# Eight PSUM banks divided anew in a two-layer diffusion backbone: three for the score products, none for transposes alone

## The chip, the cores and the metric

The kernel runs on one core of a Trainium2 chip. The metric is the time on the device in microseconds (us), the median of several executions. The text speaks of the core's engines by the profile's names: PE is TensorE (matmuls and transposes, results in PSUM alone), PEld its loading of weights, DVE is VectorE, ACT is ScalarE, POOL is GpSimd, SP is the engine that issues most DMAs. PSUM has eight banks of 128 partitions by 512 float32 values in this kernel, and it uses all eight.

## What is computed

Two layers over 1024 latent tokens with a prefix of 256 context tokens, width 1024. In each layer the stream is normalized and modulated, projected, mixed by two parallel branches, gated with SiLU, projected back and added. Cut to what matters:

```
for i in range(2):
    h_lat = rms_norm(x_lat, norm_g[i]) * (1 + sc_l) + sh_l      # the same for the context
    if i == 0:   # A: global attention, 8 heads, RMS-normed and rotated q, k;  B: windowed, with a sink
        q, k, v, gate = split(h @ w_in);  q, k = rope(norm(q)), rope(norm(k))
        o = softmax(q k^T / 8 + bias) v
        y = (o * silu(gate)) @ w_out
    else:        # C: convolution module;  D: 2-D neighbourhood attention with a bias table
        ...
    x = x + g * y
return rms_norm(x_lat, final_g)
```

The output is the normalized latent stream, 1024 by 1024.

## The kernel before

Everything stands transposed, with features on the partitions and tokens along the free axis. A matmul that must be exact is written as three matmuls of split operands (`mm3`, L317 to L320: high by high, high by low, low by high), so a projection of one 128 by 512 block takes 8 x 3 = 24 matmuls into one bank.

**Stages.** First the modulation vectors and the normalization of the three token chunks; then the projections of the first head group alone ("solo"). Then layer 0's attention: 40 groups (four head groups `u` in the order 2, 3, 0, 1, ten query blocks each; 2 and 3 are branch B, 0 and 1 branch A), between whose steps the projections of the next head group are woven in as fill, and later the parts of the output projection. Then layer 1's convolution with its projections, layer 1's attention (16 groups) with more projections woven in, and the last norm.

**Order of the work.** A main generator (`attn_gen`, L392) and a fill generator are stepped by `weave` (L495): so many fill steps to so many main steps. The traced instructions carry a priority; those of the fill stand 80 places later in layer 0 (`FL`, `later`), the modulation steps 100 places (`LATE`). The framework then orders the instructions of each engine by priority and by when their inputs come in a modelled run; on the chip every engine goes through its own list in that order. Memory tiles have tags: a tag has a fixed number of buffers, and its tiles take them in turn, in the order of the program, each waiting until the buffer's last tenant is released.

**The banks.** `bank(tag, name)` (L103) takes a PSUM bank. Before, the eight banks are: `pp` two (projections: tiles `pq`, `pg`, `p1`, `po`), `mx` two (the products whose maxima are wanted), `st` two (score products), `ov` one (the product of the probabilities with V), `tr` one. While `solo` is set, a request for `pp` alternates in pairs between `pp` and `mx`.

**One group of attention.** `attn_prep` (L364) loads q, computes a bound on every query's scores (`maxes`: PE products into `mx`, DVE reductions L578, L589, L597, L1344, L1351), and then turns the negated maxima (`nmt`) with a transpose into the row layout (tile `trn`, L386 to L388), which DVE writes into rows 64 and on of `QL`. The main loop makes a score tile (`st`, L465 and L469; the second matmul adds the maxima through `QL`), ACT takes the exponential (`pf`, L477; in layer 1 DVE first adds a bias, L474), ACT casts the high part `ph` (L296), POOL or DVE subtracts for the low part `pl` (L299), and some tiles later three matmuls add to `ov` (L409 to L411).

**One head group's projection.** `proj_qkv` (L789) makes ten blocks, `pq`, each 24 matmuls; ACT copies each to `pc` (L802), a buffer for two blocks of which there are three (`PCB`). DVE and POOL normalize and rotate `pc`. Some blocks later `qk_tail` (L834) transposes the block into the tile `trk` (three transposes, L838), splits it (ACT L296 and DVE L299 into `qs`), stores q and k with two DMAs (L841, L842) and starts the loads of K and V. The last reading of a `pc` buffer is the transposes of its two blocks. `proj_gate` makes the gate blocks, `pg`.

**The other users of `tr`.** `rstd_steps` (L244) sums squares with small matmuls (`trs`); `mod_half` and `mod_half_v` (L169, L193) bring the modulation vectors into columns (`trm`), which DVE reads at L187 and L226. In the solo stage `mod_half_v` uses `ov` for it.

Of the kernel before, what the change touches and what calls it, by code (L numbers as in the profile page):

```python
# [41 lines left out]
TRV = "pp"  # L42
# [45 lines left out]
def tile_kernel(ctx: ExitStack, tc: tile.TileContext, a, out):  # L88
# [5 lines left out]
    dp = ctx.enter_context(tc.tile_pool(name="dp", bufs=1, space=DRAM))  # L94
    ps = ctx.enter_context(tc.tile_pool(name="ps", bufs=2, space=PSUM))

    BUFS = {"pp": 2, "mx": 2, "st": 2, "ov": 1, "tr": 1}
    solo = [True]
    turn = [0, 0]
    mk, mwp, hold, layer = [0], [None], [0], [0]  # L100
# [10 lines left out]
    def nm(s):  # L111
        uid[0] += 1
        return f"{s}_{uid[0]}"
# [55 lines left out]
    def mod_half(pool, l, part, j):  # L169

        pb = bank("pp", nm("pm"))
        c0 = part * 1024 + j * 512
        for d2 in range(4):
            w2 = mw_tile()
            mm0.append(SY.dma_start(w2, a["mod_w"][l, 2 * d2 * P : (2 * d2 + 2) * P, c0 : c0 + 512].rearrange("(d p) n -> p d n", d=2)))
            for d in range(2):
                dk = 2 * d2 + d
                PE.matmul(pb[0:2, :], csil[:, dk, :], w2[:, d, :], start=(dk == 0), stop=(dk == DK - 1))
        row = a0.tile([P, 512], F32, tag="ost", name=nm("mrow"), bufs=2)[0:2, :]
        SC.copy(row, pb[0:2, :])  # L180
        tr = bank("tr", nm("trm"))
        for i in range(4):
            PE.transpose(tr[:, 2 * i : 2 * i + 2], row[:, i * P : (i + 1) * P], ident[0:2, 0:2])
        trv = tr[:, 0:8].rearrange("p (i c) -> p i c", c=2)
        o = part * 8 + j * 4
        dst = modT[l][:, o : o + 4, :]
        VE.tensor_tensor(dst, trv, modb[:, l, o : o + 4, None].broadcast_to([P, 4, 2]), op=ALU.add)  # L187
        if part == 1:
            VE.scalar_tensor_tensor(gs[l][:, j * 4 : j * 4 + 4, :], dst, 1.0,
                                    normg[:, l, j * 4 : j * 4 + 4, None].broadcast_to([P, 4, 2]),  # L190
                                    op0=ALU.add, op1=ALU.mult)

    def mod_half_v(pool, l, part, j, conds):  # L193
# [26 lines left out]
            yield  # L220
        o = part * 8 + j * 4
        for n_, (q, t) in enumerate(zip(conds, accs)):
            tr = bank("ov" if solo[0] else "tr", nm("trm"))
            for i in range(4):
                PE.matmul(tr[:, 2 * i : 2 * i + 2], t[:, i * P : (i + 1) * P], one, start=True, stop=True)
            VE.tensor_tensor(modT[l][:, o : o + 4, q], tr[:, 0:8].rearrange("p (i c) -> p i c", c=2)[:, :, 0],  # L226
                             modb[:, l, o : o + 4], op=ALU.add)
            if part == 1:
                js = slice(j * 4, j * 4 + 4)
                VE.scalar_tensor_tensor(gs[l][:, js, q], modT[l][:, o : o + 4, q], 1.0, normg[:, l, js],  # L230
                                        op0=ALU.add, op1=ALU.mult)
# [9 lines left out]
        VE.scalar_tensor_tensor(r[:, :n], t[:, :n], 1.5, r[:, :n], op0=ALU.add, op1=ALU.mult)  # L241
        return r

    def rstd_steps(pool, accs, n, tag, inv=1.0, tr="tr"):  # L244


        nb = n // P
# [116 lines left out]
    def attn_prep(pool, g):  # L364
# [18 lines left out]
            VE.tensor_tensor(nmt[:, 8:12], se, nmt[:, 4:8].bitcast(F32), op=ALU.subtract)  # L383
        for _ in range(3):
            yield
        tr2 = bank("tr", nm("trn"))  # L386
        PE.transpose(tr2[0:nr, 0:P], nmt[:, 0:nr].bitcast(F32), ident)
        VE.tensor_tensor(QL[64 : 64 + nr, :].rearrange("p (h q) -> p h q", h=4),  # L388
                         tr2[0:nr, None, 0:P].broadcast_to([nr, 4, P]),
# [262 lines left out]
    with ExitStack() as p0x:  # L652
# [6 lines left out]
        with tc.tile_pool(name="st0", bufs=1, reuse_waits="tile") as st0:  # L659
# [30 lines left out]

            def norm_bc(c, acc):
                n = CHUNKS[c][1]
                return run(rstd_steps(st0, [acc], n, "st"))[:, :n]

            made = [0]
            accs, bcs, mh = [], [], [(0, 0), (0, 1), (1, 0), (1, 1)]
# [136 lines left out]

        def qk_tail(u, j, pc):  # L834

            tr = bank("tr", nm("trk"))
            for i in range(3):
                PE.transpose(tr[:, i * P : (i + 1) * P], pc[:, i * P : (i + 1) * P], ident)  # L838
            qs = ap.tile([P, 2, 384], F32R, tag="qs", name=nm("qs"), bufs=2)
# [130 lines left out]
    with tc.tile_pool(name="o0", bufs=1, reuse_waits="tile", side="right") as op_:  # L970
# [47 lines left out]
        accs = {}  # L1018
# [46 lines left out]
        weave(main, O1[2], chain(load_oh(parts[1]), out0_part(parts[1])), 30, False)  # L1065
        ws = [load_w(op_, a["ev_wo"], e2 * 256, 256, 256, WO, lambda dk: "gv"[dk % 2], dks=final, rb=2) for e2 in range(4)]
        fp = [final_proj(c) for c in range(3)]
        nh = [norm_h(0, "st", "tr"), norm_h(1, "pp", "tr"), norm_h(2, "st", "tr")]
        weave(main, NSTEP[U1 // 2] - O1[0] - O1[1] - O1[2], through_attention(), O1[3])
        a0x.close()  # L1070
        solo[0] = True
# [27 lines left out]
    with ExitStack():  # L1099
# [25 lines left out]
        def ln_steps(vp, c):  # L1125
# [23 lines left out]
                    VE.tensor_tensor(s1, s1, sq, op=ALU.add)  # L1149
                yield  # L1150
            yield
            bc = yield from rstd_steps(vp, [s1], 512, "st", 2.0)
            SC.copy(s2, bc)
            yield
            for i in range(4):
# [478 lines left out]
```

## Time and profile before

| | |
|---|---|
| median of three executions | 1557.82 us (1554.83 to 1560.38) |
| profiled execution | 1555.72 us, span of its instructions 1553.9 us |
| mean granted clock of TensorE | 0.967 |
| moved by DMA | 221.01 MB |

The profiled execution lies 2.1 us under the median of the three. The profile gives for each engine the busy time, the waits by what ended them, and the instructions in order of time. "PE st L465 <- ACT pf L477: 16.5, 17, 2.3" reads: PE stood idle ahead of the matmul of line 465 that writes `st`, and what ended the wait was ACT's instruction of line 477 that writes `pf`; 16.5 us in total, 17 times, 2.3 us the longest. In a table of windows each engine has its busy time and the number of its instructions, then follow the granted clock of TensorE as a share of full speed, the share of DMA time and GB/s.

### The profile page before, as it was taken

To read this page: it belongs to the slowest core of one execution; us is meant where nothing else is said; L and a number is where in the kernel's file an instruction comes from. 1 tells how busy PE (TensorE), PEld (TensorE's weight loads), DVE (VectorE), ACT (ScalarE), POOL (GpSimd) and SP (SyncE) were. 2 spreads that over 40 slices of the span, in tenths; PEclk is the share of its full clock that TensorE was granted. 3 is DMA by queue.
4 is the path that set the end of the run, shared out by engine and by line. 5 is a ranking of instruction groups with operands and counts; after the bars stand their busy time and mean duration, and the time that the engine had idled before them with its cause. 6 is when DMAs were issued, how large, how long until landed. Compare 5 with 4: busy or idle time off the path is not lost.

```text
span 1553.9 us, 22052 instructions
## 1 busy us (share of the span) xinstructions
PE 1449.1 (93%) x6984; PEld 1172.3 (75%) x6984; DVE 1123.3 (72%) x2172; ACT 759.8 (49%) x1545; POOL 833.5 (54%) x762
## 2 busy tenths in 40 slices
PE   6989989999999989899999889999999999799995
PEld 1878868887789678678887668888787787687784
DVE  4998898689858666654577677999755457586776
ACT  2721354445454755565455555443434455545563
POOL 1561464555555676675455666664542443545574
PEclk9999999999999999999999999999999999899996
DMA  9548245423441124631111121213456888788623
GB/s 339 194 146 270 79 125 174 147 64 121 151 129 44 54 89 143 207 115 56 42 45 35 68 95 57 80 63 123 158 178 222 272 225 263 221 264 240 192 92 109
DMA packets 185614, 221.01 MB, mean 142 GB/s; under 512 B 17421, under 2 KB 139481, under 8 KB 185497
## 3 DMA queue, kind: packets, MB, share of 16 engines
q1 hardware_dynamic: 178832, 208.03, 43.1%
q10 hardware_dynamic: 6664, 11.57, 2.3%
q8 instruction: 55, 0.90, 0.2%
q14 instruction: 63, 0.51, 0.1%
HBM read 159.51 MB, written 60.03 MB: 141 GB/s over the span
## 4 chain that ended last, share of the span: by engine, by line
PE 67%; DVE 12%; DMA 11%; issue 3%; POOL 3%; ACT 2%; SPq 2%; DVEq 0%; ACTq 0%; POOLq 0%
PE p L320 6%; PE p L318 6%; PE p L319 6%; PE ov L409 4%; PE ov L410 4%; PE ov L411 4%; PE st L465 4%; PE po L318 4%; PE st L469 4%; PE po L319 4%; PE po L320 4%; PE pq L320 2%; PE pq L319 2%; PE pq L318 2%; DMA mw<-in_mod_w_dram 2%
## 5 line engine op out<-in xcount | busy, mean ns | idle before, releaser
L299 POOL TENSOR_TENSOR pl<-pf,ph 128x512 fp32r<-128x512 f32 (+4 forms) x321 | 399.9, 1258 | 270.7 <-ACT ph L296 218.9
L299 POOL TENSOR_TENSOR wl<-wr,wh 128x256 fp32r<-128x256 f32 (+2 forms) x256 | 197.7, 788 | 227.9 <-ACT wh L296 203.3
L477 ACT ACTIVATE pf<-st 128x512 f32<-128x512 f32 x284 | 166.2, 596 | 161.7 <-PE st L469 106.3
L296 ACT CAST ph<-pf 128x512 fp32r<-128x512 f32 (+4 forms) x364 | 209.2, 588 | 25.5 <-PE ov L410 17.6
L296 ACT CAST wh<-wr 128x256 fp32r<-128x256 f32 (+2 forms) x264 | 103.2, 404 | 172.2 <-DMA wr<-in_od_d_dram 39.3
L318 PE MATMUL p<-hh,wh 128*128 128x512 f32 x448 | 177.7, 399 | 3.7 <-DVE spk L299 1.4
L319 PE MATMUL p<-hl,wh 128*128 128x512 f32 x448 | 177.9, 398 | 0.2 <-POOL hl L299 0.2
L320 PE MATMUL p<-hh,wl 128*128 128x512 f32 x448 | 175.2, 399 | 0.1
L465 PE MATMUL st<-QH,KAt 128*128 128x512 f32 (+4 forms) x364 | 144.0, 397 | 19.8 <-ACT pf L477 16.5
L409 PE MATMUL ov<-ph,Vt 128*128 128x512 f32 (+4 forms) x364 | 143.6, 394 | 8.8 <-DVE y L631 6.4
L411 PE MATMUL ov<-pl,Vt 128*128 128x512 f32 (+4 forms) x364 | 143.7, 395 | 3.9 <-POOL pl L299 3.8
L410 PE MATMUL ov<-ph,Vt 128*64 128x512 f32 (+4 forms) x364 | 140.8, 387 | 0.0
L469 PE MATMUL st<-QL,KBt 68*128 68x512 f32 (+4 forms) x364 | 138.2, 388 | 0.8 <-DVE QL L388 0.7
L1116 DVE SCALAR_TENSOR_TENSOR cps<-U,taps,cps 128x512 f32<-128x512 f32 x184 | 124.3, 747 | 0.0
L589 DVE TENSOR_REDUCE mp<-mx 128x1 f32<-128x512 f32 x128 | 85.5, 682 | 33.5 <-PE mx L588 32.7
L219 DVE SCALAR_TENSOR_TENSOR macc<-mw,csil,macc 128x512 f32<-128x512 f32 x107 | 97.5, 929 | 14.0 <-DMA mw<-in_mod_w_dram 13.2
L318 PEld LDWEIGHTS p<-hh,wh 128*128 128x128 f32 x448 | 84.6, 189 | 24.5 <-DVE spk L299 1.6
L465 PEld LDWEIGHTS st<-QH,KAt 128*128 128x128 f32 x364 | 69.8, 192 | 42.5 <-ACT pf L477 25.3
L319 PEld LDWEIGHTS p<-hl,wh 128*128 128x128 f32 x448 | 84.6, 189 | 20.4 <-POOL hl L299 0.6
L320 PEld LDWEIGHTS p<-hh,wl 128*128 128x128 f32 x448 | 84.6, 189 | 20.3 <-POOL wl L299 1.0
L411 PEld LDWEIGHTS ov<-pl,Vt 128*128 128x128 f32 x364 | 71.1, 195 | 28.1 <-POOL pl L299 7.6
L409 PEld LDWEIGHTS ov<-ph,Vt 128*128 128x128 f32 x364 | 71.5, 196 | 24.3 <-issue 7.0
(277 smaller groups left out, 3518.4 us busy)
## 6 DMA issues: line engine op xcount, KB each, us to landing
mw<-in_mod_w_dram SPq DMA_DIRECT2D x34, 512.0 KB, 5.6
bs<-in_d_bs_dram SPq DMA_DIRECT2D x16, 832.0 KB, 7.3
Q<-qs SPq DMA_DIRECT2D x40, 256.0 KB, 2.7
QH<-Q SPq DMA_DIRECT2D x80, 128.0 KB, 2.7
bm<-in_d_bm_dram SPq DMA_DIRECT2D x16, 540.0 KB, 6.1
wr<-in_od_d_dram SPq DMA_DIRECT2D x64, 128.0 KB, 2.6
mw<-in_mod_w_dram SPq DMA_DIRECT2D x28, 256.0 KB, 3.1
wr<-in_ev_qkv_dram SPq DMA_DIRECT2D x32, 192.0 KB, 3.8
```

The lines of the kernel that those rows point to most:

```text
L296: SC.copy(hi, src)
L299: (GP if leng == "g" else VE).tensor_tensor(lo, src, hi.bitcast(F32), op=ALU.subtract)
L318: PE.matmul(o, lh, rh, start=first, stop=False)
L319: PE.matmul(o, lh, rl, start=False, stop=False)
L320: done[0] = PE.matmul(o, ll, rh, start=False, stop=last)
L409: PE.matmul(o, V[:, 64:192], ph[:, :n], start=(t == 0), stop=False)
L410: PE.matmul(g.ov[0:64, q0 : q0 + n], V[:, 0:64], ph[:, :n], start=False, stop=False)
L411: pvs.append(PE.matmul(o, V[:, 64:192], pl[:, :n], start=False, stop=(last and g.sink is None)))
L465: sts.append(PE.matmul(st[:, :n], KA[:, cs], g.QH[:, q0 : q0 + n], start=True, stop=False))
L469: PE.matmul(st[:, :n], KB[0:68, cs], g.QL[0:68, q0 : q0 + n], start=False, stop=True)
L477: SC.activation(pf[:, :n], st[:, :n], AF.Exp, scale=1.0 if g.bias else SCALE)
L1116: VE.scalar_tensor_tensor(pc, uc, w, pc, op0=ALU.mult, op1=ALU.add)
```

## The change

The tag `tr` goes, and `st` gets its bank. The tiles that had `tr` move as follows: the transposes of `qk_tail` to `pp` (the constant `TRV` is "pp"), those of the maxima (`trn`), the modulation sums outside the solo stage and the sums of squares by default to `mx`, the modulation row of `mod_half`, the sums of squares of the first norms and of the layer norm to `st`. Nothing else is changed: the same instructions on the same data.

```diff
-    BUFS = {"pp": 2, "mx": 2, "st": 2, "ov": 1, "tr": 1}
+    BUFS = {"pp": 2, "mx": 2, "st": 3, "ov": 1}
...
     def mod_half(pool, l, part, j):
...
-        tr = bank("tr", nm("trm"))
+        tr = bank("st", nm("trm"))
...
     def mod_half_v(pool, l, part, j, conds):
...
-            tr = bank("ov" if solo[0] else "tr", nm("trm"))
+            tr = bank("ov" if solo[0] else "mx", nm("trm"))
...
-    def rstd_steps(pool, accs, n, tag, inv=1.0, tr="tr"):
+    def rstd_steps(pool, accs, n, tag, inv=1.0, tr="mx"):
...
     def attn_prep(pool, g):
...
-        tr2 = bank("tr", nm("trn"))
+        tr2 = bank("mx", nm("trn"))
...
             def norm_bc(c, acc):
...
-                return run(rstd_steps(st0, [acc], n, "st"))[:, :n]
+                return run(rstd_steps(st0, [acc], n, "st", tr="st"))[:, :n]
...
         def qk_tail(u, j, pc):
...
-            tr = bank("tr", nm("trk"))
+            tr = bank(TRV, nm("trk"))
...
-        nh = [norm_h(0, "st", "tr"), norm_h(1, "pp", "tr"), norm_h(2, "st", "tr")]
+        nh = [norm_h(0, "st", "mx"), norm_h(1, "pp", "mx"), norm_h(2, "st", "mx")]
...
-            bc = yield from rstd_steps(vp, [s1], 512, "st", 2.0)
+            bc = yield from rstd_steps(vp, [s1], 512, "st", 2.0, "st")
```

## The prediction, made before the changed kernel ran

> **What bounds the kernel now.** I read the page first, then PE's waits, then tables of windows over layer 0, then the order of time in them. The page:
>
> ```profile
> span 1553.9 us, 22052 instructions
> PE 1449.1 (93%) x6984; PEld 1172.3 (75%) x6984; DVE 1123.3 (72%) x2172; ACT 759.8 (49%) x1545; POOL 833.5 (54%) x762
> PE 67%; DVE 12%; DMA 11%; issue 3%; POOL 3%; ACT 2%; SPq 2%; DVEq 0%; ACTq 0%; POOLq 0%
> ```
>
> PE is the bound: two thirds of the chain that ended last are its own work, and no change of banks takes a matmul away. The change can only work on the 104.8 us (1553.9 less 1449.1) in which PE stands idle, and on stretches in which its clock is halved. PE's waits, over the span:
>
> ```profile
> PE st L465 <- ACT pf L477: 16.5, 17, 2.3
> ...
> PE trk L838 <- DVE qs L299: 6.6, 5, 2.8
> PE ov L409 <- DVE y L631: 6.4, 4, 5.1
> ...
> PE ov L411 <- POOL pl L299: 3.8, 3, 3.2
> ...
> PE st L465 <- DVE pf L474: 2.8, 3, 1.8
> ```
>
> The largest single wait is the first score matmul of a tile: it needs no result of the exponential, so what it waits for is the bank that the exponential (or in layer 1 the bias sum) still reads. That is 16.5 + 2.8 = 19.3 us in 20 waits. The second row is the other single bank that the change touches: a transpose waits until the last `trk` has been read. The same first wait in the windows 150 to 350, 350 to 500 and 500 to 650 us:
>
> ```profile
> PE st L465 <- ACT pf L477: 4.2, 4, 2.1
> PE st L465 <- ACT pf L477: 2.0, 4, 1.2
> PE st L465 <- ACT pf L477: 5.1, 5, 2.2
> ```
>
> So 11.3 of it lie in the attention with projections woven in. There the trace shows something that the table of waits doesn't name. In the third head group, in order of time (DVE, PE three times, ACT):
>
> ```profile
> 465.68 1.31 DVE L816 TENSOR_TENSOR pc<-pc,gain 128x640 f32<-128x640 f32 x1
> ...
> 479.99 0.27 PE L387 MATMUL trn<-ident,nmt 128*4 128x128 f32 x1
> ...
> 503.80 0.34 PE L320 MATMUL pq<-wh,hl 128*128 128x384 f32 x1
> ...
> 504.21 0.27 PE L387 MATMUL trn<-ident,nmt 128*4 128x128 f32 x1
> ...
> 520.67 0.27 PE L387 MATMUL trn<-ident,nmt 128*4 128x128 f32 x1
> ...
> 521.95 0.28 PE L838 MATMUL trk<-ident,pc 128*128 128x128 f32 x1
> ...
> 542.40 0.86 ACT L802 COPY pc<-pq 128x384 f32<-128x384 f32 x2
> ```
>
> The first two blocks (context tokens, not rotated) are normalized at 467.0, yet their first transpose runs at 521.95, 55 us later and right behind a `trn`. Between the `trn` rows lie 24.2 and 16.5 us, so the bank was mostly empty. It was not its turn: `tr` has one bank, its tiles take it in program order, and the program has those `trn` first. Until the two transposes have run, no `pc` buffer comes free; so the projections that ended at 504 hold both `pp` banks until the double copy at 542.40, and the fill stands still. Such stretches, from the projection that finds no bank to the next copy, or to the next tail:
>
> ```profile
> 176.00:210.00 34.00, 30.26 (x142) 22.82 (x140) 29.58 (x68) 17.90 (x40) 18.45 (x15) 0.90 0.23 68
> 212.00:237.00 25.00, 22.64 (x111) 18.77 (x110) 23.15 (x49) 13.25 (x37) 17.61 (x16) 0.93 0.49 148
> 341.00:370.00 29.00, 25.85 (x118) 17.90 (x116) 26.41 (x60) 15.81 (x36) 17.06 (x13) 1.00 0.30 89
> 384.00:397.00 13.00, 10.98 (x64) 8.72 (x64) 12.72 (x27) 7.18 (x19) 8.72 (x9) 1.00 0.44 137
> 504.00:542.00 38.00, 35.11 (x151) 24.40 (x150) 23.44 (x45) 26.64 (x46) 26.52 (x21) 1.00 0.16 48
> 555.00:578.00 23.00, 18.15 (x69) 12.55 (x68) 13.20 (x27) 11.77 (x24) 14.98 (x14) 0.85 0.25 73
> ```
>
> Columns: length, PE, PEld, DVE, ACT, POOL with their counts, granted clock, DMA share, GB/s. PE's idle time here sums to 3.74 + 2.36 + 3.15 + 2.02 + 2.89 + 4.85 = 19.0 us, and the clock lost is 0.10 x 34 + 0.07 x 25 + 0.15 x 23 = 8.6 us. How the two hang together, around the worst one (ACT, PE three times, a window):
>
> ```profile
> 559.14 0.40 ACT L296 CAST wh<-wr 128x256 fp32r<-128x256 f32 x1 [4.23 <-DMA wr<-in_ev_g_dram]
> ...
> 560.61 0.50 PE L465 MATMUL st<-QH,KAt 128*128 128x512 f32 x1 [2.19 <-ACT pf L477]
> ...
> 563.07 0.51 PE L576 MATMUL mx<-KAt,QH 128*128 128x256 f32 x2 [1.21 <-DVE mp L589]
> 564.22 0.80 PE L465 MATMUL st<-QH,KAt 128*128 128x512 f32 x1 [0.64 <-ACT pf L477]
> ...
> 564.00:571.00 7.00, 6.78 (x18) 4.94 (x19) 1.59 (x4) 3.71 (x8) 4.71 (x6) 0.55 0.26 77
> ```
>
> ACT stood 4.23 us behind a weight that hadn't landed, the exponentials behind it waited, both score banks stayed full, PE idled 2.19, 1.21 and 0.64 us, and then ran seven microseconds at 0.55 of its clock.
>
> **The change part by part.** The sum is against the profiled execution's 1555.72 us.
>
> *Third score bank.* When a score tile meets two full banks, PE now goes on with it and with the products and `ov` matmuls queued behind it, until the next score tile. Bounds: the whole 19.3 us, or nothing, where the idle time comes back at the next instruction whose input the same late ACT or POOL makes (`ov` on `pl`, a row above: 3.8 us already). The exponential has two `pf` buffers as before, so ACT isn't faster. In the case shown, some four of PE's instructions stood between the first stalled score and the next blocked one, about 1 us of a 2.19 us wait. I take that share, a half: -9.
>
> *Clock.* If the idle halves, the half-clock stretches that follow should too; bounds 0 and 8.6: -4.
> The Trainium skill, in "TensorE: Matmul & The Clock Gate", section "HAM oscillation — how this bites in real kernels", puts the throttling at idle gaps over about 3.4 us; by it none of these single gaps would cost clock, and the sum would lose this -4. Here gaps of 2.19, 1.21 and 0.64 us within 4 us did (0.55 in the row above), which is closer to the page's next section, on micro-idles between groups when PSUM banks cycle.
>
> *Transposes of q and k to `pp`.* Their place in the turn is now between projections of the same fill; no `trn` stands ahead. The 55 us wait goes, `pc` comes free early, and the fill flows through the six stretches, which are covered at present by attention alone. Of their 19.0 us of idle time 11.3 at most are the score waits already counted; the rest, 7.7, can be filled, bounds 0 and 7.7: -4. The tail's DMAs (two stores each, and the loads of K and V behind blocks 1, 5 and 9) are issued on SP's queue earlier by as much; the loads of the next head group then have more time ahead of their use, and what they pass are q loads of 128 KB, which I cost at nothing.
>
> *What it costs in `pp`.* The two banks go in turn: from the fifth block on the program has projection, tail, projection, tail, so that all projections get one bank and all tails the other. A projection then waits for the copy of the last one, five times in each of three head groups. The prices:
>
> ```profile
> L802 ACT COPY pc<-pq x40: 461/480/514, 64.6 to 578.2; 128x384 f32<-128x384 f32 x40
> ...
>   PE pq L320: 40.9, 13
> ...
> L296 ACT CAST qs<-trk x40: 460/478/492, 77.3 to 639.4; 128x384 fp32r<-128x384 f32 x40
> L299 DVE TENSOR_TENSOR qs<-trk,qs x40: 510/554/559, 87.3 to 639.9; 128x384 fp32r<-128x384 f32 x40
> L388 DVE TENSOR_TENSOR QL<-trn,k_bd x56: 681/682/684, 178.2 to 1490.8; 4x512 fp32r<-4x512 f32 x36, 12x512 fp32r<-12x512 f32 x20
> ...
> 190.82 0.95 PE L225 MATMUL trm<-one,macc 128*128 128x2 f32 x8
> ...
> 195.42 0.16 DVE L226 TENSOR_TENSOR modT<-trm,modb 128x4 f32<-128x4 f32 x1
> ```
>
> In 13 of 40 cases ACT was waiting for the projection and the copy took its 0.48 us at once; in the others ACT was busy, at worst as in the 4.23 us above. So a copy costs 0.48 to 4.7 us, 15 of them 7 to 71 us if nothing hid them. Behind a blocked projection PE's list holds scores and `ov` matmuls of the attention, which have priority over the fill, but the list is in order: what stands behind waits too. In the modelled order such a wait is seen and attention put ahead of it, so I take 0.4 us each: +6. The tail itself, 0.48 + 0.55 us after its transposes, delays only the next tail, as before.
>
> *What it costs in `mx`.* `trn` stands in turn with the maxima, so only one product of the next group can run until DVE's 0.68 us at L388 is done; a group's maxima are due some tiles ahead, so most of that is hidden. The modulation sums are worse: outside the solo stage they come in pairs, wait for late DVE work, and block both banks; from the matmuls at 190.82 to their reading at 195.42 are 4.6 us. There are four such places (two pairs, two single): 0 to 18 us, mostly ahead of its due time: +3.
>
> *The rest.* In the solo stage the transposes share four banks, and the 6.6 us of the `trk` wait may go; but a projection there follows the second one before it in its bank instead of the fourth, and pays copies. Bounds -6.6 and, with five copies at 0.48, +2.4; I take 0, as DVE is as busy there. Sums of squares in `mx` and `st`: those tags are idle when they run, 0; if not, they wait one 0.68 us read in some eleven places, +7 at most, and below nothing they can gain no more than the `trk` row.
>
> Sum: -9 -4 -4 +6 +3 = -8, so 1555.72 - 8 = 1547.7, forecast 1548. By the median of the runs shown, 2.1 above the profiled execution, it would be 1550; the difference is inside the spread of those runs.
>
> **The rivals.**
>
> *Projections in one bank (slower).* For it: the alternation is certain, and the copies stand in ACT's queue behind casts and exponentials; two of three found ACT busy. Against it: attention has priority and work to give. Price: five copies at 0.48 and ten at half the 4.23 us wait plus 0.48 = 2.4 + 26 = 28 us, of which PE can fill perhaps a third, as the attention alone leaves PE idle in the stretches above: +19, with the -8 - 6 of the rest still gained (the +6 is in the 19): 1556 + 19 - 14 = 1561. It decides as soon as a projection's wait costs PE more than 0.9 us on average (14 / 15).
> The Trainium skill says, in "Perfetto Trace Analysis", section "Matmuls", that independent groups should rotate through different banks so that emptying one overlaps the next group's matmuls; this change ends that for these blocks. With every copy exposed at its 0.48 us that rule would make the term 7 and not 6.
>
> *Nothing moves.* The idle time passes from the bank to the next input: ACT was late for a DMA, and a third tile in front of it makes it no earlier; the fill that flows early is missing later, when attention runs alone. For it: no bank makes ACT or POOL faster. Then -3 to +3: 1556. That the change doesn't do what it says, a third bank seldom used as `pf` stays at two buffers, ends here too.
>
> *All of it.* All 19.3 us of waits, the 8.6 of clock and the 7.7 go, at the costs above: -35.6 + 9 = 1529. Against it: two thirds of the score waits come from a late ACT.
>
> **How the numbers follow.** The forecast's mechanism, with a gain of over 4.7 us (0.3%, about what a measurement of this kernel can tell from no change): 0.43; all of it: 0.07; nothing moves, within 0.3%: 0.23; projections in one bank, slower by over 0.3%: 0.27, which includes costs in `mx` at their upper end. So faster 0.50, same 0.23, slower 0.27. The range goes from 1534, some two thirds of the way to the whole gain, to 1567, the slower rival with a third of the 18 us in `mx` on top; outside lie one in ten on each side. The forecast's own range is 1538 to 1551.
>
> **What would show it.** In the profile after: the row "st L465 <- ACT pf" at half of 16.5 or less; the first tail of the third head group within some microseconds of its projections, and the double copies of `pc` gone; PE's idle time in layer 0's first 500 us smaller; the granted clock above 0.967. Against it: new waits of `pq` L318 on ACT L802 of over 6 us in sum, waits of `mx` matmuls on L388 or L226, or the score waits come back as waits of `ov` on `pl` and `ph`. I am wrong if the score waits fall and the span doesn't, or if the fill still stands behind `trk`.

## The result and the profile after

The change made the kernel slower: 1619.32 us median (1615.64 to 1622.15, four executions) against 1558.13 (1554.83 to 1560.38, four executions) for the kernel before, a ratio of 1.0393 with a 95% interval of 1.0362 to 1.0424. The forecast was 1548 with a range up to 1567. The profiled execution after took 1617.21 us; before, 1555.72. The page after:

```profile
span 1615.4 us, 21980 instructions
PE 1477.5 (91%) x6984; PEld 1189.5 (74%) x6984; DVE 1120.6 (69%) x2172; ACT 767.2 (47%) x1545; POOL 830.7 (51%) x762
PE 65%; DVE 14%; DMA 10%; issue 5%; POOL 3%; ACT 2%; SPq 1%; ACTq 0%; DVEq 0%; POOLq 0%
```

The 61.5 us by which the span grew are two things. PE is busy 28.4 us longer with the same 6984 matmuls, so they took longer, and PE is idle 33.1 us longer (137.9 against 104.8). The mean granted clock fell from 0.967 to 0.946. PE's waits after, to be held against the first list of the prediction:

```profile
...
PE trn L387 <- DVE nmt L383: 9.8, 7, 2.9
PE st L465 <- ACT pf L477: 8.8, 6, 4.6
PE mx L588 <- DVE mp L589: 7.7, 11, 2.4
...
PE trk L838 <- DVE qs L299: 6.1, 4, 2.6
...
PE mx L576 <- DVE QL L388: 4.7, 4, 2.1
PE trk L838 <- DVE nmt L377: 4.4, 1, 4.4
...
PE st L465 <- DVE pf L474: 2.6, 4, 1.5
...
PE pq L318 <- ACT pc L802: 2.2, 1, 2.2
```

The row on which the prediction rested did nearly what was asked of it: the wait for a score bank is 8.8 us instead of 16.5 (half of that, 8.25, or less was asked). In its place stand rows that were absent or small before: PE waits for the maxima (`trn` on `nmt`), and maxima products wait for DVE's reading of a `trn` (`mx` L576 on L388).

**Where in the kernel.** Windows cut at the same work in both kernels: up to the first score product, to the first projection of layer 1, to the first score of layer 1, to the last score, to the end. Columns: length, PE, PEld, DVE, ACT, POOL with their counts, granted clock, DMA share, GB/s. Before:

```profile
0.00:159.40 159.40, 135.19 (x678) 105.63 (x679) 127.86 (x205) 58.34 (x123) 58.16 (x55) 0.94 0.72 238
159.40:923.60 764.20, 723.60 (x3505) 586.75 (x3504) 549.96 (x1072) 402.39 (x806) 455.32 (x375) 0.98 0.31 97
923.60:1213.30 289.70, 285.15 (x1315) 231.04 (x1314) 212.07 (x350) 121.15 (x237) 151.07 (x155) 1.00 0.41 132
1213.30:1516.30 303.00, 284.87 (x1388) 230.90 (x1387) 207.52 (x486) 166.33 (x353) 150.54 (x160) 0.97 0.75 220
1516.30:1553.90 37.60, 20.31 (x106) 17.99 (x104) 25.87 (x61) 11.56 (x28) 18.44 (x19) 0.68 0.31 112
```

After:

```profile
0.00:162.00 162.00, 136.53 (x676) 106.84 (x677) 128.18 (x208) 58.40 (x123) 58.43 (x55) 0.93 0.71 234
162.00:963.20 801.20, 742.53 (x3501) 595.99 (x3499) 545.10 (x1068) 407.97 (x804) 450.36 (x375) 0.94 0.30 92
963.20:1262.40 299.20, 288.06 (x1303) 233.24 (x1302) 213.33 (x352) 120.73 (x235) 150.23 (x152) 0.98 0.39 126
1262.40:1563.80 301.40, 279.05 (x1360) 226.26 (x1359) 200.40 (x476) 161.48 (x342) 146.62 (x158) 0.97 0.74 222
1563.80:1615.40 51.60, 31.38 (x152) 27.16 (x150) 33.59 (x72) 18.64 (x42) 25.03 (x24) 0.72 0.25 88
```

Layer 0's attention with its fill has 37 of the 61.5 us (801.2 less 764.2): 18.9 busy at a clock of 0.94 instead of 0.98, and 18.1 idle. The stretch after it has 9.5, the tail behind the last score 14.0, the rest 1.0.

Inside layer 0 the two streams have drifted apart. Before, the 20th `trn` runs at 448.6 us and the last gate projection, the end of the projection fill, at 637.4. After, the 20th `trn` runs at 540.0, 91 us late, and the last gate projection ends at 564.8, 73 us early: attention lags, the fill runs ahead, and afterwards attention has to run with less beside it. Over the stretch with projections, 162 to 564.8 us, the first rows of PE's waits after are:

```profile
PE trn L387 <- DVE nmt L383: 9.8, 7, 2.9
PE trk L838 <- DVE nmt L377: 4.4, 1, 4.4
PE mx L576 <- DVE QL L388: 3.4, 2, 2.1
PE mx L596 <- DVE mp L597: 3.1, 3, 1.7
```

Before, in the same stretch (159 to 637.4), the first row was the score wait:

```profile
PE st L465 <- ACT pf L477: 10.3, 12, 2.2
```

After, it is 0.4 us there. Fewer scores come that could fill the banks: PE starts 87 score tiles in these 402.8 us, 21.6 in 100 us; before it was 148 in 478.0 us, 31.0 in 100 us.

**What became slow.** One group's preparation, after (PE's products, DVE's reductions, the transpose, and the next group's first products):

```profile
310.85 0.55 DVE L597 CUSTOM_DVE_ANT_0 mx<-mx,k_bm 128x384 f32<-128x384 f32 x1
...
311.50 0.17 DVE L377 TENSOR_REDUCE nmt<-mp 128x4 fp32r<-128x12 f32 x1
...
316.04 0.27 PE L387 MATMUL trn<-ident,nmt 128*12 128x128 f32 x1
...
316.07 0.48 PE L576 MATMUL mx<-KAt,QH 128*128 128x256 f32 x2
...
317.97 0.68 DVE L388 TENSOR_TENSOR QL<-trn,k_bd 12x512 fp32r<-12x512 f32 x1
...
321.19 0.40 PE L576 MATMUL mx<-KAt,QH 128*128 128x256 f32 x2
```

The last maximum is reduced at 311.4 (310.85 + 0.55), both of the maxima's banks are empty, and PE has fill to do; yet no product of the next group runs until the `trn` at 316.04 has taken its bank, 4.6 us later. The second pair can't run before DVE has read the `trn` (at 318.65), and runs at 321.19. Before, at the same point of the work:

```profile
236.69 0.63 PE L576 MATMUL mx<-KAt,QH 128*128 128x256 f32 x4
...
237.61 1.28 DVE L578 TENSOR_REDUCE mp<-mx 128x2 f32<-128x512 f32 x2
...
240.57 0.27 PE L387 MATMUL trn<-ident,nmt 128*12 128x128 f32 x1
...
241.51 0.34 PE L596 MATMUL mx<-KAt,QH 128*128 128x384 f32 x1
```

Four products of the next group have run and two of its reductions are done before the `trn` of this one. The order in which PE ran the tiles of maxima (m) and the transposes (T), up to the twelfth T, shows it for the first groups:

```
before:  mmmmmmmmTmmmmmmmTmmmmmTmmTmmmmmmmTmmmmmTmmTmmmmmmmmmmmmTmmmmmmTmmTmmTmmmmmmmmT
after:   mmmmmmTmmmmmmTmmmmmmTmmTmmmmmmTmmmmmmTmmTmmmmmmTmmmmmmTmmmmmmTmmmmmmTmmmmmmT
```

These are groups of branch B: each has six tiles of maxima, or two in the two groups of context tokens. After, each T closes its group before the next group's first m. The tiles of a tag take its banks in the program's order, and the program has this `trn` ahead of the next group's maxima.

Three numbers from the instruction records of groups 3 to 20, all of branch B, serve below. *Length* is the mean time from a group's first reduction (L578) to the end of its writing of `QL` (L388). *Distance* is the mean time between two such ends. *Overlap* counts the groups, of these 18, whose successor's first reduction starts before their own `trn`. Before: length 24.0, distance 14.7, overlap 15. After: 18.7, 18.6, 0. A single preparation got shorter; but now one begins when the last has ended, so the distance is the length. Attention is late because its groups come every 18.6 us instead of every 14.7.

### The profile page after: what moved, and what is told of

Same layout as the page of the kernel before. It is cut to its first block, busy times and chain, and to the rows that moved or that the text cites. A ratio compares the mean times of both kernels' runs of the same rounds, so it can differ in the third digit from the quotient of the medians.

```text
span 1615.4 us, 21980 instructions
## 1 busy us (share of the span) xinstructions
PE 1477.5 (91%) x6984; PEld 1189.5 (74%) x6984; DVE 1120.6 (69%) x2172; ACT 767.2 (47%) x1545; POOL 830.7 (51%) x762
## 4 chain that ended last, share of the span: by engine, by line
PE 65%; DVE 14%; DMA 10%; issue 5%; POOL 3%; ACT 2%; SPq 1%; ACTq 0%; DVEq 0%; POOLq 0%
PE p L318 6%; PE p L319 6%; PE p L320 6%; PE ov L409 4%; PE ov L411 4%; PE ov L410 4%; PE po L318 4%; PE po L319 4%; PE po L320 3%; PE st L465 3%; PE st L469 3%; PE pq L320 2%; PE pq L318 2%; PE pq L319 2%; DVE macc L219 2%
## 5 line engine op out<-in xcount | busy, mean ns | idle before, releaser
L299 POOL TENSOR_TENSOR pl<-pf,ph 128x512 fp32r<-128x512 f32 (+4 forms) x321 | 394.8, 1242 | 336.3 <-ACT ph L296 279.4
L299 POOL TENSOR_TENSOR wl<-wr,wh 128x256 fp32r<-128x256 f32 (+2 forms) x256 | 201.5, 803 | 199.9 <-ACT wh L296 188.0
L477 ACT ACTIVATE pf<-st 128x512 f32<-128x512 f32 x284 | 166.7, 597 | 170.6 <-PE st L469 97.7
L465 PE MATMUL st<-QH,KAt 128*128 128x512 f32 (+4 forms) x364 | 143.4, 397 | 11.8 <-ACT pf L477 8.8
L469 PE MATMUL st<-QL,KBt 68*128 68x512 f32 (+4 forms) x364 | 134.3, 395 | 1.2 <-DVE QL L388 1.2
L465 PEld LDWEIGHTS st<-QH,KAt 128*128 128x128 f32 x364 | 70.7, 195 | 31.7 <-ACT pf L477 13.3
```

The costliest lines, as they stand in the source:

```text
L299: (GP if leng == "g" else VE).tensor_tensor(lo, src, hi.bitcast(F32), op=ALU.subtract)
L465: sts.append(PE.matmul(st[:, :n], KA[:, cs], g.QH[:, q0 : q0 + n], start=True, stop=False))
L469: PE.matmul(st[:, :n], KB[0:68, cs], g.QL[0:68, q0 : q0 + n], start=False, stop=True)
L477: SC.activation(pf[:, :n], st[:, :n], AF.Exp, scale=1.0 if g.bias else SCALE)
```

## The experiments

The first theories: (1) the transposes of q and k (`trk`), free of the turn that they had with `trn`, let the fill run ahead and attention is overtaken; (2) `trn` and the sums, in turn with the maxima, stretch attention's preparation; (3) the third score bank is itself harmful. From e5 on, theory A is (2) and theory B is (1). Each ratio is to the kernel before on the same chip, with its 95% interval.

| label | us | ratio | length / distance / overlap | 20th `trn` late by |
|---|---|---|---|---|
| after | 1619.3 | 1.0393 (1.0362-1.0424) | 18.7 / 18.6 / 0 | 91 |
| e1_st_two | 1611.8 | 1.0327 (1.0276-1.0379) | 18.1 / 18.2 / 0 | 79 |
| e2_tails_own_bank | 1604.4 | 1.0266 (1.0227-1.0305) | 18.5 / 18.4 / 0 | 91 |
| e3_tails_in_pp | 1577.1 | 1.0092 (1.0055-1.0129) | 19.4 / 14.5 / 13 | 8 |
| e4_maxima_transposes_in_mx | 1593.3 | 1.0204 (1.0160-1.0248) | 18.4 / 18.9 / 0 | 93 |
| e5_three_maxima_banks | 1587.0 | 1.0168 (1.0125-1.0211) | 15.9 / 15.8 / 0 | 32 |
| e6_trn_with_scores | 1622.8 | 1.0387 (1.0363-1.0412) | 18.3 / 14.9 / 9 | 23 |
| e7_sums_in_mx | 1572.7 | 1.0066 (1.0042-1.0089) | 22.9 / 15.2 / 11 | 14 |
| e8_trn_in_mx_fill_held | 1627.6 | 1.0421 (1.0395-1.0447) | 16.8 / 17.0 / 0 | 48 |
| e9_tails_in_pp_pairs | 1579.8 | 1.0126 (1.0105-1.0147) | 19.6 / 14.4 / 14 | 11 |
| e10_pairs_alone | 1577.8 | 1.0116 (1.0094-1.0138) | 26.4 / 15.6 / 14 | 15 |
| e11_single_bank_joined_to_maxima | 1597.8 | 1.0239 (1.0208-1.0270) | 15.7 / 16.0 / 0 | 33 |
| e12_trn_behind_next_maxima | 1571.3 | 1.0079 (1.0050-1.0108) | 21.2 / 15.8 / 18 | 40 |
| e13_changed_trn_behind_next_maxima | 1594.3 | 1.0233 (1.0204-1.0261) | 22.4 / 16.0 / 18 | 40 |
| e14_e13_with_two_score_banks | 1597.8 | 1.0246 (1.0218-1.0275) | 23.3 / 16.3 / 18 | 42 |
| e15_edit_on_before | 1577.6 | 1.0115 (1.0079-1.0151) | 27.1 / 15.8 / 15 | 21 |
| e16_three_maxima_banks_and_order | 1586.2 | 1.0175 (1.0133-1.0218) | 21.4 / 15.0 / 14 | 15 |

The medians of the kernel before beside these runs were 1558.1 to 1562.1 us.

### The parts of the change

e1, the changed kernel without the third score bank:

```diff
-    BUFS = {"pp": 2, "mx": 2, "st": 3, "ov": 1}
+    BUFS = {"pp": 2, "mx": 2, "st": 2, "ov": 1}
```

> The changed kernel with two score banks again; the eighth bank stays unused. Theory 1 (the tails of q and k, freed from the turn of the maxima's transposes, let the projections run ahead of the attention, which is left alone later): 1610 to 1625, as the changed kernel. Theory 2 (the maxima's transposes and the modulation sums stand in turn with the maxima and stretch the attention's preparation): the same, 1610 to 1625. Theory 3 (the third score bank itself makes the order worse): 1555 to 1575. If the third bank gives what I forecast for it, 9 to 13 us, this kernel is at 1630.

The loss stays: 50 us against 61. The third bank is not what hurts, and it gains nothing either; theory 3 falls as the main cause. The score waits of e1, with two banks as before:

```profile
PE st L465 <- ACT pf L477: 10.6, 13, 2.5
...
PE st L465 <- DVE pf L474: 4.0, 6, 2.0
```

14.6 us instead of 19.3: 4.7 of the 7.9 us by which the two rows fell in the changed kernel (to 8.8 + 2.6) come without the third bank, which the prediction wanted to prove by the first of them. Here too the scores come thinly: 86 tiles in the 400.2 us up to the last gate projection.

e2, as e1, with the eighth bank for the transposes of q and k alone:

```diff
-    BUFS = {"pp": 2, "mx": 2, "st": 3, "ov": 1}
+    BUFS = {"pp": 2, "mx": 2, "st": 2, "ov": 1, "tr": 1}
...
-            tr = bank(TRV, nm("trk"))
+            tr = bank("tr", nm("trk"))
```

> The changed kernel with two score banks, and the eighth bank for the transposes of q and k alone; those of the maxima and the small sums stay in the banks of the maxima. The tails are free of the attention's turn here too. Theory 1: about as the changed kernel, 1605 to 1625. Theory 2: the same, 1605 to 1625. If projections that share two banks with the tails are what costs (the slower rival of the prediction): 1560 to 1580.

1604, a hair under the range of both theories and 42 us over the kernel before: far from the 1560 to 1580 of the slower rival. Against e1 it is 7 us less, with intervals that overlap, so the projections' banks carry little of the loss here.

e3 and e4, the kernel before with one move each:

```diff
-            tr = bank("tr", nm("trk"))
+            tr = bank(TRV, nm("trk"))
```

```diff
-        tr2 = bank("tr", nm("trn"))
+        tr2 = bank("mx", nm("trn"))
```

> The kernel before with one move alone: the transposes of q and k go to the projections' banks; the maxima's transposes and the sums keep the bank tr. Theory 1: the whole loss of layer 0, 1595 to 1615, with the last gate block near 565 us instead of 637 and the first attention groups 30 to 90 us late. Theory 2: no slower than before, 1545 to 1560.

> The kernel before with one move alone: the transposes of the maxima go to the banks of the maxima; the tails and the sums keep the bank tr, so the tails are free of the attention's turn here as well, but for the modulation sums. Theory 1: slower, 1585 to 1615. Theory 2: slower too, 1580 to 1610, with waits of maxima products on line 388 as in the changed kernel (4.7 us of PE). If neither holds: 1555 to 1560.

e3 costs 15 us, e4 31: the move that the prediction held nearly free is the dear one. e3 is a miss for both theories, as 1577 lies between their ranges; e4 lies in the ranges of both. In e3 the tails are as free as in the changed kernel, but the fill is not ahead (its last gate projection ends 12 us late) and attention is 8 us late: free tails alone don't let the fill overtake. e4 by itself shows the whole displacement: the 20th `trn` 93 us late, overlap 0.

e7, the modulation sums alone:

```diff
-            tr = bank("ov" if solo[0] else "tr", nm("trm"))
+            tr = bank("ov" if solo[0] else "mx", nm("trm"))
```

> The kernel before with one thing changed: in the woven part the transposing sums of the modulation (trm) take the maxima's banks; trn, trk and the sums of squares stay in the single bank. Theory A: the sums wait for late work of DVE with a maxima bank in hand, eight of them, some 4 us each: 1562 to 1575 with the first groups late by up to 15 us. Theory B: no tail moves, so 1555 to 1561.

11 us, inside A's range and outside B's; the trace has six such sums in the woven part, not eight. What that is worth is limited by e10 below.

### Is it the turn of the maxima, or the fill that runs ahead?

e5, as e1 with the eighth bank for the maxima:

```diff
-    BUFS = {"pp": 2, "mx": 2, "st": 3, "ov": 1}
+    BUFS = {"pp": 2, "mx": 3, "st": 2, "ov": 1}
```

> The changed kernel with two score banks and the eighth bank given to the maxima (three banks for the maxima, trn and the sums between them); the transposes of q and k stay in the projections' banks, so beside e1_st_two only that one bank differs. Theory A (trn and the sums stand in the maxima's turn, each group's preparation gets longer, attention falls behind): with three banks two maxima can be in work beside a waiting trn, so trn 19 comes 25 to 60 us late instead of 79, and the time is 1575 to 1595. Theory B (the tails, free of trn's turn, let the projections run ahead, and attention is merely overtaken): the tails are as free as in e1, so the time stays at 1605 to 1618 and trn 19 near +79.

1587 and 32 us late, both as A has it. Preparations still don't overlap, but with three banks one takes 15.9 us instead of 18.1.

e6, the changed kernel with `trn` in the scores' banks:

```diff
-        tr2 = bank("mx", nm("trn"))
+        tr2 = bank("st", nm("trn"))
```

> The changed kernel with trn in the three banks of the scores instead of the maxima's two; everything else as changed. Theory A: the maxima are free of trn, only the modulation sums still stand in their turn: 1575 to 1590, trn 19 late by 20 to 50 us. Theory B: the tails are as free as in the changed kernel: 1605 to 1620, trn 19 near +91. A rival to A that puts the whole loss on sharing any turn with the scores or maxima: no gain, 1610 and more.

A miss for A's time: the 20th `trn` is 23 us late, as A has it, and the distance is 14.9, but the time is 1623. The loss has moved. The first score product runs at 188.66 us, right behind the second `trn` (188.63), instead of at 159.4 as before; from there to the first projection of layer 1 it takes 765.1 us, as before (764.2). So a `trn` that waits for its maxima holds up the scores that stand behind it in a common turn too, and the third rival that was written down for this run has the time right. Layer 1 and the tail add 37 us, whose cause was not traced.

e8, e4 with the fill held to attention (the argument that `weave` has for it, in four calls):

```diff
-            weave(main, n - n0 - NLAST[u // 2], fill0(k + 1), NFILL[k], False)
+            weave(main, n - n0 - NLAST[u // 2], fill0(k + 1), NFILL[k], False, True, 2)
```

> As e4 (the kernel before with trn in the maxima's banks, 1593), and the woven projections of layer 0 held back so that none is issued before the score tile that stands two tiles ahead of it in the program: the projections can't run ahead of attention. Theory A: attention's preparation is still stretched by the shared turn, and now PE has nothing to put in its place: idle time of PE rises, 1580 to 1605, trn 19 still 30 us late or more. Theory B: with the projections held, attention comes back to its old times (trn 19 within 10 us) and the time to 1556 to 1570. A mixed result (attention back, but the time over 1570) would mean that holding costs by itself.

B falls. With the fill unable to run ahead (its last gate projection ends at 727.0 us, 90 us later than before), the 20th `trn` is still 48 us late: the fill running ahead is not what makes attention late. The time is 34 us worse than e4's, over A's range, and PE is idle 25.2 us longer than in e4 (148.0 against 122.8). Whether the fill had saved part of the loss in e4, or the hold costs that by itself, is open: the hold alone, on the kernel before, was not run.

### The tails, and a control

e9, as e3 with the tails in pairs, and e10, the kernel before with the tails in pairs and no bank changed:

```diff
-                    if len(tails) > 2:
-                        qk_tail(*tails.pop(0))
+                while len(tails) > 2:
+                    qk_tail(*tails.pop(0))
```

> As e3 (the kernel before with the transposes of q and k in the projections' banks, 1577), but the tails in pairs behind each second projection: the program's turn is then projection, projection, tail, tail, and projections use both banks again. Theory C (the loss of e3 is that its projections all stand in one bank behind ACT's copy, the prediction's slower rival): 1558 to 1568. Theory D (it is the tail itself that holds a projection bank while it waits for the normalizing and rotating of its block, whichever order): 1572 to 1582, as e3.

> Control for e9: the kernel before, with the tails in pairs as in e9, all banks as before. Both theories: the tails have a bank apart from the projections, so only their order changes: 1555 to 1565. If it is slower than that, pairs cost by themselves and e9 is read against this kernel.

e9 by itself is in D's range and out of C's. But the control came out against what both had for it: a mere change of the tails' order, with every bank as before, costs 17 us. The expectation says what follows then, that e9 is to be read against the control. So read, the tails in the projections' banks cost 2 us, with intervals that overlap, once the pairs let projections use both banks, and that is what C had. As the price of the pairs need not be the same in both kernels, neither C nor D is shown. The page of e10:

```profile
PE 1465.0 (93%) x6984; PEld 1179.9 (75%) x6984; DVE 1128.1 (71%) x2172; ACT 761.2 (48%) x1545; POOL 830.2 (53%) x762
```

PE is busy 15.9 us longer than before at the same work, its mean granted clock is 0.958 instead of 0.967, and it is idle 9.9 us longer (span 1579.7). So an edit that only moves the order loses up to 17 us here, in these two executions more than half of it by longer busy time at a lower clock, and the 15 us of e3 and the 11 of e7 can't be told from that. The 31 us of e4 can.

e11, the kernel before with its single bank joined to the maxima's two, all its tiles in one turn of three:

```diff
-    BUFS = {"pp": 2, "mx": 2, "st": 2, "ov": 1, "tr": 1}
+    BUFS = {"pp": 2, "mx": 3, "st": 2, "ov": 1}
```

> The kernel before with its single bank added to the maxima's two: three banks in one turn for maxima, trn, trk and the sums. No third score bank, no tail in the projections' banks. Theory A: what counts is whether a second group's maxima can run while a trn waits; with three banks they can, though only behind trn in the turn, and the tails now stand in that turn too: 1560 to 1585. If the common turn is harmless with three banks, 1555 to 1562; if the third bank is worth more than the coupling costs, below 1555.

1598, over every range written for it: a common turn isn't harmless with three banks. Overlap 0 again, and here the transposes of q and k stand in that turn as well.

### The place in the turn

e12 is e4 with the `trn` put behind the first two tiles of the next group's maxima. Banks, tiles and work are those of e4, and a preparation starts two tiles earlier:

```diff
-LEAD = (3, 4)
+LEAD = (1, 4)
...
-        for _ in range(3):
-            yield
+        while g.hold:
+            yield "T"
         tr2 = bank("mx", nm("trn"))
...
+                if x >= len(items):
+                    groups[k].hold = 0
+                r = next(p, work)
...
+                if r == "T":
+                    if len(work) > 1 and work[1][0] <= x:
+                        next(work[1][1])
+                        groups[k].hold -= 1
+                    elif not layer[0]:
+                        return
...
```

`hold` is 2 in layer 0 (0 for the first two groups): a preparation that has come to its `trn` waits until two steps of the next one have been taken, or until its own group starts.

> As e4 (the kernel before with trn in the maxima's two banks, 1593), but in layer 0 the program puts each group's trn behind the first two maxima of the next group (and starts a preparation two tiles earlier, so that these exist by then). The banks, the chain of one group and the work are the same; only the place in the turn differs. Theory A (two preparations must overlap): the next group's maxima run while a trn waits, the tenth trn and the twentieth are 15 to 60 us late instead of 52 and 93, and the time is 1568 to 1585. Rival (the loss comes from the maxima's banks being held for the trn, wherever it stands, or from any change of order): 1588 to 1605.

1571 instead of 1593, within A's range; the tenth and the twentieth `trn` are 20 and 40 us late, also within it. The distance is 15.8 although the single preparation got longer (21.2). One `trn` of e12 with the products around it (the lines behind it have other numbers in this kernel: L591 is L576, L593 is L578):

```profile
303.45 0.40 PE L591 MATMUL mx<-KAt,QH 128*128 128x256 f32 x2
...
304.87 0.17 DVE L377 TENSOR_REDUCE nmt<-mp 128x4 fp32r<-128x12 f32 x1
...
304.90 0.48 PE L591 MATMUL mx<-KAt,QH 128*128 128x256 f32 x2
...
305.15 0.69 DVE L593 TENSOR_REDUCE mp<-mx 128x2 f32<-128x512 f32 x1
...
308.37 0.27 PE L387 MATMUL trn<-ident,nmt 128*12 128x128 f32 x1
```

The next group's two pairs run at 303.45 and 304.90, ahead of the `trn` at 308.37. The place in the turn is the cause, and not that a `trn` takes a bank from the maxima. The edit also starts a preparation two tiles earlier, and that part alone was not run; but in e4 a preparation begins when the last has ended (length 18.4, distance 18.9, overlap 0), so an earlier permission by itself would find the turn still taken. That the fill is still 70 us ahead in e12 (last gate projection at 567.3), and the whole only 13 us over the kernel before, speaks against B once more.

e13 is the same edit on the changed kernel, e14 the same with two score banks, e15 the same on the kernel before:

> The changed kernel with the same edit. Theory A: 1580 to 1600, a gain of 20 us or more on its 1619. Rival: within 8 us of 1619.

> As e13 with two score banks and the eighth bank unused (e1 with the same edit). If the third score bank is worth the 9 us that the prediction gave it, e14 is 5 to 13 us over e13; if it is worth nothing, as e1 against the changed kernel says, e14 is within 6 us of e13 or below it.

> Control: the kernel before, whose trn stands in a bank apart from the maxima, with the same edit. Here the maxima of the next group run ahead of trn anyway, so theory A expects no gain: 1556 to 1580, the upper half being the price of a changed order that e10 showed. If it were below 1552, the edit would gain by itself and e12 and e13 would have to be read against that.

e13 gains 25 us on the changed kernel. e15 shows that the edit gains nothing where the overlap was there already; it costs 19. So e12's 13 us over the kernel before are no more than the edit's own price there; if it is the same in e12, nothing is left of e4's 31. By the same reckoning e13, 36 us over the kernel before, keeps some 17 us that neither the edit's price nor the place of the `trn` in the turn accounts for.

By the measure set down for it, within 6 us of e13, e14 answers what the third score bank is worth: 3.5 us, with intervals that overlap for the most part. PE's waits for a score bank in e13 (three banks), then e14 (two); L480, L489 and L492 are L465, L474 and L477 there:

```profile
PE st L480 <- ACT pf L492: 8.7, 11, 1.8
...
PE st L480 <- DVE pf L489: 1.4, 2, 1.1
```

```profile
PE st L480 <- ACT pf L492: 15.0, 9, 7.0
...
PE st L480 <- DVE pf L489: 7.5, 4, 3.9
```

The bank takes 12.4 us of waits away, and the spans are 1597.6 and 1596.2. The pages of e13 and of e14 show where they went:

```profile
PE 1475.5 (92%) x6984; PEld 1191.5 (75%) x6984; DVE 1122.3 (70%) x2172; ACT 764.6 (48%) x1545; POOL 825.3 (52%) x762
```

```profile
PE 1465.5 (92%) x6984; PEld 1186.3 (74%) x6984; DVE 1128.0 (71%) x2172; ACT 764.8 (48%) x1545; POOL 831.7 (52%) x762
```

PE is idle 8.6 us less with three banks (122.1 against 130.7) and busy 10.0 us longer at the same work. (The profiled execution of e13 was the slowest of its four, 5 us over their median, so part of the 10.0 is that; its clock, 0.947, is like that of the other three, 0.948 and 0.949, and all four of e14 have 0.950 to 0.954.)

e16, e5 with the same edit, was the one left that might have beaten the kernel before:

> As e5 (three banks for maxima, trn and sums, two for scores, tails in the projections' banks, 1587), with trn behind the next group's first two maxima as in e12. Theory A: a third bank had already given e5 most of what the order gives, so a smaller gain than e12's 22 us: 1568 to 1582, periods of the first groups near 15 us. It beats the kernel before (1558) only if the third bank is worth more than the tails and the sums cost in their new places (15 and 11 us, each alone), which I do not expect.

A miss: the overlap is back (14) and the distance is 15.0, but the time is that of e5. Either nothing is gained between 15.8 and 15.0, and what e5 lost lies elsewhere, by the size of it in the tails and the sums (15 and 11 us, each alone); or the order gains about what the edit itself costs (19 in e15). These runs don't tell the two apart. No kernel here beats the one before.

## Why the prediction was wrong, point by point

**`trn` in `mx`: the step that failed.** The prediction: "only one product of the next group can run until DVE's 0.68 us at L388 is done; a group's maxima are due some tiles ahead, so most of that is hidden", and +3 for this and the sums together. It looked at the 0.68 us that the bank is occupied, and at the due time of one group. But the turn also makes the next group's maxima wait for the `trn` to start, 4.6 us in the case shown, and so ends the overlap of two preparations. Attention's pace was then set by the length of one preparation: 18.6 us a group instead of 14.7. It measured 31 us alone (e4), and e12 takes 22 of them back by moving the `trn` in the turn (and starting a preparation two tiles earlier). The rows for it were at hand: in the trace of before, 15 of the 18 groups have their successor's first reduction ahead of their `trn`; the prediction noted such turns for `trk` and didn't ask the same of the maxima.

**Third score bank, -9.** Measured 3.5 us in e14 against e13, which can't be told from nothing, and e1 without the bank has the smaller ratio (1.0327 against 1.0393). The wait does go, and the time doesn't. The "nothing moves" rival had that result but not the reason: it let the idle time come back at the next input, while in e13 PE's idle time is 8.6 us less than in e14, and longer busy time eats that. The row put forward as proof, half of 16.5, was nearly met in the changed kernel (8.8) and is no proof, as e1 shows. The prediction's own condition, "I am wrong if the score waits fall and the span doesn't", is what came about.

**Clock, -4.** The other way: 0.946, where above 0.967 was set down. The term took it that the clock follows the score waits; in e10 (11.7 us in that row, clock 0.958) and e13 (8.7, 0.947) it fell while they fell too. That the longer idle time of PE as a whole brought it down fits the record (last section); what in the order of the work made it so was not tested.

**Transposes of q and k to `pp`, -4 + 6.** The mechanism was right. The first tail of the third head group no longer waits for a `trn` (DVE, PE):

```profile
447.32 0.82 DVE L816 TENSOR_TENSOR pc<-pc,gain 128x640 f32<-128x640 f32 x1
...
455.33 0.49 PE L838 MATMUL trk<-ident,pc 128*128 128x128 f32 x3
```

It runs 7.2 us after its block is normalized, instead of 55. Of the five double copies of `pc` behind the solo stage one is left. No gain came of it: PE's idle time in layer 0's first 500 us rose from 29.2 to 37.3 us, where the prediction had it smaller, and e3 is 15 us slower, which is no more than a change of order alone costs (e10). The wait of `pq` on L802 is 2.2 us, under the 6 that the prediction set. Its slower rival had the sign of the result; as the main cause it is excluded by e2 (7 us less than e1), as a cause of e3's 15 us it is open (e9).

**Modulation sums.** Part of the +3; 11 us alone (e7), again within what an order costs.

**The rest, 0.** The solo stage grew by 2.6 us (162.0 against 159.4), just over the bound of 2.4; but in e4, where only the `trn` moved, it ends at 162.9, so this isn't put down to the transposes of q and k. For the end the prediction has no term: behind the last score the changed kernel takes 14.0 us more, e1 only 3.3. In the changed kernel more is left there (152 of PE's instructions against 106). What puts it there was not traced.

The terms together: `trn` 31 (e4), tails 15 (e3) and sums 11 (e7), each alone, make 57; e1, which has all three, measured 50, and the changed kernel 61. They add up roughly, but two of the three are of the size of e10's control, so only the first has a cause that is shown: 31 of the 61 us. The other half stays open.

## What to carry to other kernels

Before a tile joins a rotating set of buffers, write down the order of the program's requests around it, and ask what stands behind it in that turn while it waits for its input: the price is not only how long it occupies the buffer, but the overlap that ends. Look in the trace of before for work that runs out of the program's order; a new common turn forbids exactly that. And run a control that changes only the order: where such a control costs 1%, a row of waits that shrinks, and differences of that size, prove nothing.

## What the runs showed of the hardware

The lost time is to a good part slower matmuls, not waits. By the trace's record of the granted clock, PE was at half clock for 103.0 us of the span in 16 stretches before, and for 175.8 us in 22 stretches after; most of these last 3.4, 6.8 or 10.2 us. By the instruction records, gaps of PE over 3.4 us are only 2 before (9.1 us together) and 6 after (25.6). The Trainium skill, in "TensorE: Matmul & The Clock Gate", section "HAM oscillation — how this bites in real kernels", ties throttling to gaps over about 3.4 us. That there are more half-clock stretches where there are more such gaps agrees; that there are eight times as many stretches as such gaps before does not, so shorter gaps must count too.

The record shows more. The stretches of a trace start on one grid of 3.41 us. Take each interval of this grid that itself ran at full clock (but for the first 12 us of PE's work and the last 9 us) and add up PE's gaps in it. With more than 1.8 us of idle time in sum, half clock followed in 7 of 7 intervals before and in 12 of 12 after; with 0.9 to 1.8 us in 7 of 20 and 8 of 20; with less in 1 of 392 and 1 of 383. Over all 18 traces of this case these are 209 of 215, 132 of 396 and 16 of 6922. So in these traces it is the sum of the gaps within such an interval that tells, not one long gap. In the prediction's example the stretch began at 563.5 us, behind the gaps of 2.19 and 1.21 us; the one of 0.64 us came after that.

Fewer idle microseconds over the whole span didn't mean a higher clock: e13 against e14 has 8.6 us less idle time and a clock of 0.947 against 0.954. Why is open.

The Trainium skill also says, in "Perfetto Trace Analysis", section "Matmul Optimizations", that all eight PSUM banks should be in use. The runs here don't bear that out by itself: e1, with a bank unused, took 1611.8 us, and the changed kernel with all eight 1619.3; the kernel before, also with all eight, took 1558.1. Which tiles share a turn decided here, not the number of banks in use.
